# Two plain FFN blocks become a fourth group of seven products

## The chip, the core and the metric

The kernel runs on one core of a Trainium2 chip. The metric is the device time of one execution in microseconds (us), as the median of the runs. The engines are TensorE (PE: matmuls; PEld: its weight loads), VectorE (DVE), ScalarE (ACT), GpSimd (POOL) and SyncE (SP), which here only issues transfers. Each engine works through its own queue of instructions in the order in which the program put them there.

## What is computed

The reference is a trunk of two layers over 256 tokens of width 1024, in float32: a gated linear attention branch beside a grouped-query attention branch, a merge, then a SwiGLU feed-forward network (FFN) and a small embedding step, each with its norms. Cut to the FFN, which the change touches, with h of 256 x 1024 and a hidden width of 2816:

```python
u = rms_norm(h, g_ffn_pre)
gate, up = jnp.split(u @ w_ffn_in, 2, axis=-1)     # w_ffn_in: 1024 x 5632
h = h + rms_norm((jax.nn.silu(gate) * up) @ w_ffn_out, g_ffn_post)
```

## The kernel before

**Arithmetic.** Every float32 operand is held as two halves: a high half that TensorE takes (fp32r) and the remainder, the low half. A product of two operands is three matmuls: high by high, high by low, low by high (`mm3`, and the inner loop of `times`).

**The stream of weights.** Weights come in units of 1 MB (128 partitions x 2048 floats), in one list for the whole kernel, the *plan*. Class `Stream` handles them. `start` issues the next load on SyncE (L263) as soon as there is a place for it. `split` (L113, L109) makes the two halves, in two pieces each: a cast on ScalarE into `wh`, then on VectorE the subtraction that gives `wl`. The pool has four pairs of `wh` and `wl`; `fill` makes the next unit whenever fewer than four are held, and `done` gives a pair back when TensorE has used it.

**The FFN.** The hidden width is cut into 11 blocks of 256. A plain block is two units, one for each half of the rows, with the block's gate and up columns side by side; each takes 24 matmuls. Two blocks together can be done as a *group of seven products* (`seven`, L581): a scheme for 2 x 2 block matrices with seven half-sized products in place of eight, at the price of sums. A product is 12 matmuls, a group 84, two plain blocks 96. The sums on the activations are made once per layer (`sums`). The sums on the weights are made for every group, in `Stream.step`. With x, z, y and q the four units of a group:

- product 1 uses x; then VectorE adds z to x (L292) and a DMA adds y to z (L295)
- product 2 uses x; then VectorE adds y to x (L292)
- product 3 uses x; then two accumulating transfers issued by GpSimd add q, read from memory anew, to x (L308)
- products 4, 5, 6 and 7 use y, z, q and x

x and z are loaded straight into a `wh` and a `wl` buffer (tag `lent`), and so take one of the four pairs. They are loaded only after the previous group's product 7 has been made (`self.lend`, set in `step` for n = 7). y is loaded into another buffer, and q into a `raw` buffer like a plain unit, at the place of product 5 in the list of loads.

**Order.** A string sets the order of the units within the FFN, and the same string sets it in the plan: `u` is a unit of a plain block, a digit a product of a group, `o` a unit of `w_ffn_out` (24 matmuls, which need the hidden activations of that block, turned by a copy on ScalarE, a transposing transfer, another copy, and a cast with its low half), and `p` loads a gain and the embedding input, with no unit. PLAIN and PAIRS name the blocks (a pair by its first block; blocks 0 and 1 are done ahead of the string), OUT the order of the output units. The engines' queues follow from the order in which this code emits its instructions, with small tasks of other work woven in at ticks; when the program is built, instructions whose data allow it are also moved past one another, so the final queues are shown below where they matter.

The evictions of a group's products, by ScalarE's copies in `seven`, are L629 (product 1), L632 (product 2) and L634 (product 3); VectorE takes the later ones. `vmul` (L106) makes silu(gate) x up.

## Time and profile before

| | us |
|---|---|
| median of 3 runs | 918.69 |
| lowest and highest run | 918.22, 921.97 |
| the profiled execution | 921.25 |
| its span, first to last instruction | 919.1 |

The profile is of one execution. Its parts give the busy time of each engine, the chain of work that ended last (followed back from the last instruction through what released each step), the costliest groups of instructions, and the transfers. A timeline row has its start, its duration, the engine, the line of the kernel, the operation with output <- input, the count, and in brackets the idle time before it with what ended that. A name such as `wl_0ffnin` is the tile's tag and the part of the program: `0ffnin` is the FFN's first matrix in layer 0, `1ffnin` in layer 1. In rows with a count of 2 the duration runs over both.

### The profile page before, as it was taken

Reading aid. Unit: us, or ns where it says so; the run is one execution under the profiler, and the core shown is the slowest. Engines: PE = TensorE matmul, PEld = TensorE weight load, DVE = VectorE, ACT = ScalarE, POOL = GpSimd, SP = SyncE. Lnnn points to the kernel's source line nnn. Section 1 sums busy time; section 2 is a strip of 40 time slices with the busy share of each in tenths; the row PEclk is TensorE's granted clock in tenths of the full one; section 3 lists DMA queues with packets and bytes.
Section 4 is the critical chain, followed back from the end, with each engine's and each line's share of the span. In section 5 each row is a group of like instructions: output and inputs, shape, how many; then the busy total and the mean of one; then the engine's idle time right before and its main releaser. Section 6 shows DMA issues by size and latency. Waiting matters only on the chain.

```text
span 919.1 us, 12313 instructions
## 1 busy us (share of the span) xinstructions
PE 904.6 (98%) x4561; PEld 768.3 (84%) x4561; DVE 737.2 (80%) x947; ACT 643.9 (70%) x1032; POOL 112.4 (12%) x174
## 2 busy tenths in 40 slices
PE   8999999999999999999999999999999999999996
PEld 6999888888888888888899988888888788878786
DVE  4798987977679796888689789688786798968874
ACT  4658777964568796776665686878656787957663
POOL 2410201140010100010023002111001010101000
PEclk9999999999999999999999999999999999999999
DMA  6555356986489998966555524399675999979541
GB/s 218 182 193 180 117 163 231 229 241 234 144 243 256 279 273 250 301 194 240 184 176 184 190 91 148 128 290 234 208 247 173 274 230 290 261 284 243 200 167 46
DMA packets 123290, 193.38 MB, mean 210 GB/s; under 512 B 33431, under 2 KB 56471, under 8 KB 122206
## 3 DMA queue, kind: packets, MB, share of 16 engines
q1 hardware_dynamic: 117726, 175.81, 59.3%
q0 software_dynamic: 5504, 16.78, 10.1%
q8 instruction: 36, 0.59, 0.3%
q14 instruction: 24, 0.20, 0.1%
HBM read 175.80 MB, written 1.05 MB: 192 GB/s over the span
## 4 chain that ended last, share of the span: by engine, by line
PE 80%; ACT 6%; DMA 5%; DVE 4%; issue 2%; POOL 2%; SPq 0%; POOLq 0%; ACTq 0%; DVEq 0%
PE acc_0ffnin L97 10%; PE acc_1ffnin L97 10%; PE acc_0ffnin L581 5%; PE acc_1gate L97 5%; PE acc_0gate L97 5%; PE acc_1ffnin L581 4%; PE acc_1gqk L97 3%; PE acc_0rq L97 2%; PE acc_0gqk L97 2%; PE acc_1ple L97 2%; PE acc_1gg L97 2%; PE acc_0gg L97 2%; PE acc_0v L97 2%; PE acc_1v L97 2%; PE acc_1merge L97 2%; PE acc_0merge L97 2%
## 5 line engine op out<-in xcount | busy, mean ns | idle before, releaser
L97 PE MATMUL acc_1ffnin<-wh_1ffnin,big_1ffnin 128*128 128x512 f32 x176 | 56.5, 392 | 0.1
L97 PE MATMUL acc_0ffnin<-wh_0ffnin,big_0ffnin 128*128 128x512 f32 x176 | 56.2, 391 | 0.0
L109 DVE TENSOR_TENSOR wl_1ffnin<-raw_1ffnin,wh_1ffnin 128x1024 fp32r<-128x1024 f32 x38 | 44.9, 1220 | 12.3 <-ACT wh_1ffnin L113 12.3
L109 DVE TENSOR_TENSOR wl_0ffnin<-raw_0ffnin,wh_0ffnin 128x1024 fp32r<-128x1024 f32 x38 | 44.9, 1221 | 10.5 <-ACT wh_0ffnin L113 10.2
L113 ACT CAST wh_1ffnin<-raw_1ffnin 128x1024 fp32r<-128x1024 f32 x38 | 38.3, 1050 | 17.7 <-DMA raw_1ffnin<-in_w_ffn_out_dram 9.1
L113 ACT CAST wh_0ffnin<-raw_0ffnin 128x1024 fp32r<-128x1024 f32 x38 | 38.4, 1050 | 16.8 <-DMA raw_0ffnin<-in_w_ffn_out_dram 7.8
L109 DVE TENSOR_TENSOR wl_1ffnin<-lent_1ffnin,wh_1ffnin 128x1024 fp32r<-128x1024 f32 x30 | 35.5, 1220 | 4.9 <-ACT wh_1ffnin L113 4.7
L109 DVE TENSOR_TENSOR wl_0ffnin<-lent_0ffnin,wh_0ffnin 128x1024 fp32r<-128x1024 f32 x30 | 35.5, 1221 | 4.8 <-ACT wh_0ffnin L113 4.7
L97 PEld LDWEIGHTS acc_1ffnin<-wh_1ffnin,big_1ffnin 128*128 128x128 f32 x176 | 33.0, 188 | 7.2 <-ACT wh_1ffnin L113 0.5
L97 PEld LDWEIGHTS acc_0ffnin<-wh_0ffnin,big_0ffnin 128*128 128x128 f32 x176 | 33.0, 188 | 6.9 <-DVE big_0ffnin L109 0.2
L113 ACT CAST wh_1ffnin<-lent_1ffnin 128x1024 fp32r<-128x1024 f32 x30 | 30.3, 1049 | 8.6 <-issue 2.9
L113 ACT CAST wh_0ffnin<-lent_0ffnin 128x1024 fp32r<-128x1024 f32 x30 | 30.3, 1050 | 8.4 <-issue 2.9
L97 PE MATMUL acc_1ffnin<-wl_1ffnin,big_1ffnin 128*128 128x512 f32 x88 | 34.4, 391 | 0.8 <-DVE wl_1ffnin L109 0.8
L97 PE MATMUL acc_0ffnin<-wl_0ffnin,big_0ffnin 128*128 128x512 f32 x88 | 34.5, 392 | 0.3 <-DVE wl_0ffnin L109 0.3
L581 PE MATMUL acc_0ffnin<-wh_0ffnin,mid_0ffnin 128*128 128x512 f32 x96 | 31.0, 390 | 0.0
L581 PE MATMUL acc_1ffnin<-wh_1ffnin,mid_1ffnin 128*128 128x512 f32 x96 | 31.0, 390 | 0.0
L97 PE MATMUL acc_0ffnin<-wh_0ffnin,big_0wout 128*128 128x512 f32 x96 | 30.4, 389 | 0.0
L97 PE MATMUL acc_1ffnin<-wh_1ffnin,big_1wout 128*128 128x512 f32 x96 | 30.3, 389 | 0.0
L97 PE MATMUL acc_0rq<-wh_start,big_start 128*128 128x384 f32 (+1 forms) x96 | 25.4, 350 | 1.5 <-ACT big_start L124 1.5
L97 PE MATMUL acc_1rq<-wh_0ple,big_0ple 128*128 128x384 f32 (+1 forms) x96 | 23.5, 325 | 0.0
L581 PE MATMUL acc_1ffnin<-wh_1ffnin,big_1wout 128*128 128x512 f32 x72 | 23.1, 389 | 0.0
L581 PE MATMUL acc_0ffnin<-wh_0ffnin,big_0wout 128*128 128x512 f32 x72 | 23.1, 389 | 0.0
(745 smaller groups left out, 3011.7 us busy)
## 6 DMA issues: line engine op xcount, KB each, us to landing
raw_0ffnin<-in_w_ffn_out_dram SPq DMA_DIRECT2D x11, 1024.0 KB, 5.1
raw_1ffnin<-in_w_ffn_out_dram SPq DMA_DIRECT2D x11, 1024.0 KB, 5.1
lent_0ffnin<-in_w_ffn_in_dram SPq DMA_DIRECT2D x6, 1024.0 KB, 7.5
lent_1ffnin<-in_w_ffn_in_dram SPq DMA_DIRECT2D x6, 1024.0 KB, 6.0
raw_0rq<-in_w_in_dram SPq DMA_DIRECT2D x4, 1024.0 KB, 5.1
raw_0v<-in_w_in_dram SPq DMA_DIRECT2D x4, 1024.0 KB, 5.1
raw_0merge<-in_w_out_dram SPq DMA_DIRECT2D x4, 1024.0 KB, 5.2
raw_0wout<-in_w_ffn_in_dram SPq DMA_DIRECT2D x8, 512.0 KB, 4.6
```

The costliest lines, as they stand in the source:

```text
L97: return nc.tensor.matmul(o, lhsT, rhs, start=start, stop=stop)
L109: nc.vector.tensor_tensor(out=out, in0=in0, in1=in1, op=ALU.subtract)
L113: cast = nc.scalar.copy(hi, src)
L581: nc.tensor.matmul(o, x, y, start=first and k + n == 0, stop=k == 3 and n == 2, skip_group_check=not first)
```

## The change

Blocks 4 and 5 leave PLAIN and become a fourth pair, so that each layer's FFN has the groups of blocks 2, 4, 6 and 8 and one plain block, 10, at the start. Between product 7 of a group and product 1 of the next there is one `o` in the new string; in the old one there were two units, `uo` and `oo`. In the groups that are listed in ADDED (the first and the last one, "far" below, with the group of the attention's output matrix) the fourth sum stays with the accumulating transfers after product 3. In the two others ("near" below) VectorE adds q to x at product 5, from q's own `raw` buffer.

```diff
@@ -35,10 +35,11 @@
 
 
 
-FFN = "uu1u2u34u567" "uo12o34o5o67" "poo12o345o67"
+FFN = "uu12o34o567" "o123o4567" "po123o4567" "o123o4567"
 MERGE = "GGGG1G2G34G5G67gggg"
-PLAIN, PAIRS = (4, 5, 10), (2, 6, 8)
-OUT = (0, 1, 2, 3, 4, 5, 10, 6, 7, 8, 9)
+PLAIN, PAIRS = (10,), (2, 4, 6, 8)
+ADDED = (2, 8)
+OUT = (0, 1, 10, 2, 3, 4, 5, 6, 7, 8, 9)
 
 WAIT_LAST = (3, 4)
 SENT, LANDED, NEXT = 3, 9, 2
@@ -172,7 +173,7 @@
             )
         ]
 
-    plan = []
+    plan, added = [], []
     for l in range(DEPTH):
         w = a["w_in"][l]
         plan += [unit_rows(w, n, C_RA, C_RA + 1056, 2 if l + n == 0 else 1) for n in range(4)]
@@ -181,6 +182,7 @@
         gates = [unit(w, kh, c0) for c0 in (C_GA, C_GA + 512, C_GB, C_GB + 512) for kh in range(2)]
         glas = [unit(a["w_o_gla"][l], kh, j * 512) for j in range(2) for kh in range(2)]
         pair = [unit(a["w_o_attn"][l], kh, j * 512) for kh in range(2) for j in range(2)]
+        added.append(id(pair))
         for x in MERGE:
             plan.append(gates.pop(0) if x == "G" else glas.pop(0) if x == "g" else (pair, int(x)))
         plan += [unit(a["w_out"][l], kh, j * 512) for kh in range(2) for j in range(2)]
@@ -193,6 +195,8 @@
         for x in FFN.replace("p", ""):
             if x == "1":
                 pair = pairs.pop(0)
+                if PAIRS[-1 - len(pairs)] in ADDED:
+                    added.append(id(pair))
             plan.append(plains.pop(0) if x == "u" else outs.pop(0) if x == "o" else (pair, int(x)))
         plan += outs
         plan += [unit_rows(a["w_ple_proj"][l], 0)]
@@ -239,7 +243,7 @@
                         self.loads += [x, y, z]
                     if n == 5:
                         self.loads.append(q)
-                    self.jobs.append(lambda p=pairs[id(units)], n=n: self.step(n, *p))
+                    self.jobs.append(lambda p=pairs[id(units)], n=n, f=id(units) in added: self.step(n, f, *p))
 
         def lent(self, tag):
 
@@ -286,7 +290,7 @@
             for piece in self.put(x):
                 self.cast = split(*piece)
 
-        def step(self, n, x, y, z, q):
+        def step(self, n, far, x, y, z, q):
             def add(to, other):
                 c = slice(0, 2048)
                 nc.vector.tensor_tensor(out=to.raw[:, c], in0=to.raw[:, c], in1=other.raw[:, c], op=ALU.add)
@@ -302,10 +306,12 @@
                 sent(z, y.raw[:, :2048])
             elif n == 2:
                 add(x, y)
-            elif n == 3:
+            elif n == 3 and far:
                 for dst, src in q.make(x.raw):
                     for c in (slice(0, 2), slice(2, 4)):
                         nc.gpsimd.dma_start(dst[:, c], src[:, c], accum_op=ALU.add)
+            elif n == 5 and not far:
+                add(x, q)
             elif n == 7:
                 self.held -= 1
                 self.lend = True
```

VectorE's queue in layer 0, at the start of the second group: in the kernel before, from the low halves for product 1 on. (`wl<-lent` is a low half from x or z, `wl<-raw` one from a unit in `raw`, `lent<-lent` a sum, `big<-mid` a piece of the turned hidden activations.)

```order
L109 TENSOR_TENSOR wl_0ffnin_483_3093<-lent_0ffnin_470_3023,wh_0ffnin_482_3092 128x1024 x2
L106 TENSOR_TENSOR t512_0ffnin_480_3087<-mid_0ffnin_437_2814,t512_0ffnin_480_3087 128x512
L292 TENSOR_TENSOR lent_0ffnin_470_3023<-lent_0ffnin_470_3023,lent_0ffnin_472_3027 128x2048
L106 TENSOR_TENSOR t512_0ffnin_462_2982<-acc_0ffnin_463_2983,t512_0ffnin_462_2982 128x256
L106 TENSOR_TENSOR t512_0ffnin_462_2982<-acc_0ffnin_464_2984,t512_0ffnin_462_2982 128x256
L109 TENSOR_TENSOR wl_0ffnin_487_3129<-lent_0ffnin_470_3023,wh_0ffnin_486_3128 128x1024 x2
L292 TENSOR_TENSOR lent_0ffnin_470_3023<-lent_0ffnin_470_3023,big_0ffnin_471_3025 128x2048
L109 TENSOR_TENSOR wl_0ffnin_495_3172<-raw_0ffnin_473_3029,wh_0ffnin_494_3171 128x1024 x2
L109 TENSOR_TENSOR big_0ffnin_501_3196<-mid_0ffnin_484_3106,big_0ffnin_501_3196 128x4x128
L109 TENSOR_TENSOR wl_0ffnin_503_3201<-lent_0ffnin_470_3023,wh_0ffnin_502_3200 128x1024 x2
```

And in the changed kernel, from the same point on (L110 is the old L109, L107 the old L106, L296 the old L292):

```order
L110 TENSOR_TENSOR wl_0ffnin_469_3013<-lent_0ffnin_462_2975,wh_0ffnin_468_3012 128x1024 x2
L296 TENSOR_TENSOR lent_0ffnin_462_2975<-lent_0ffnin_462_2975,lent_0ffnin_464_2979 128x2048
L107 TENSOR_TENSOR t512_0ffnin_472_3037<-mid_0ffnin_437_2811,t512_0ffnin_472_3037 128x512
L110 TENSOR_TENSOR wl_0ffnin_475_3043<-lent_0ffnin_462_2975,wh_0ffnin_474_3042 128x1024 x2
L296 TENSOR_TENSOR lent_0ffnin_462_2975<-lent_0ffnin_462_2975,big_0ffnin_463_2977 128x2048
L110 TENSOR_TENSOR wl_0ffnin_479_3078<-lent_0ffnin_462_2975,wh_0ffnin_478_3077 128x1024 x2
L110 TENSOR_TENSOR wl_0ffnin_485_3101<-raw_0ffnin_465_2981,wh_0ffnin_484_3100 128x1024 x2
L110 TENSOR_TENSOR wl_0ffnin_488_3122<-big_0ffnin_463_2977,wh_0ffnin_487_3121 128x1024 x2
L110 TENSOR_TENSOR big_0ffnin_489_3140<-mid_0ffnin_476_3055,big_0ffnin_489_3140 128x4x128
L296 TENSOR_TENSOR lent_0ffnin_462_2975<-lent_0ffnin_462_2975,raw_0ffnin_466_2983 128x2048
L110 TENSOR_TENSOR wl_0ffnin_491_3145<-lent_0ffnin_464_2979,wh_0ffnin_490_3144 128x1024 x2
L110 TENSOR_TENSOR big_0ffnin_489_3140<-mid_0ffnin_477_3069,big_0ffnin_489_3140 128x4x128
```

The low halves for product 3 now stand ahead of those of the output unit (`wl<-raw`), not behind them, and the sum of x and q (`lent<-lent,raw`) stands between the two pieces of the turned activations that the output unit needs.

ScalarE's queue in layer 0, from the cast for product 2 to the eviction of product 2: in the kernel before, in the second group (COPY `mid<-acc` is an eviction, CAST `wh<-lent` a cast of x, `wh<-raw` of an output unit, COPY `mid<-mid` belongs to the turning):

```order
L113 CAST wh_0ffnin_486_3128<-lent_0ffnin_470_3023 128x1024 x2
L408 COPY t512_0ffnin_488_3139<-t512_0ffnin_462_2982 128x1024
L113 CAST wh_0ffnin_494_3171<-raw_0ffnin_473_3029 128x1024 x2
L427 COPY mid_0ffnin_484_3106<-mid_0ffnin_484_3106 128x2x512
L629 COPY mid_0ffnin_497_3179<-acc_0ffnin_499_3181 128x512
L113 CAST big_0ffnin_501_3196<-mid_0ffnin_484_3106 128x4x128
L113 CAST wh_0ffnin_502_3200<-lent_0ffnin_470_3023 128x1024 x2
L427 COPY mid_0ffnin_485_3120<-mid_0ffnin_485_3120 128x2x512
L632 COPY mid_0ffnin_497_3179<-acc_0ffnin_500_3182 128x512
```

And in the changed kernel, in the third group, from the cast for product 1 to the cast of the output unit (L114 is the old L113; L635 and L638 are the old L629 and L632):

```order
L114 CAST wh_0ffnin_504_3246<-lent_0ffnin_498_3209 128x1024 x2
L1345 ACTIVATE t512_0ffnin_508_3271<-acc_0ffnin_482_3085 128x512
L414 COPY t512_0ffnin_509_3274<-t512_0ffnin_508_3271 128x1024
L635 COPY mid_0ffnin_519_3322<-acc_0ffnin_521_3324 128x512
L114 CAST wh_0ffnin_510_3276<-lent_0ffnin_498_3209 128x1024 x2
L638 COPY mid_0ffnin_519_3322<-acc_0ffnin_522_3325 128x512
L114 CAST wh_0ffnin_517_3316<-lent_0ffnin_498_3209 128x1024 x2
L114 CAST wh_0ffnin_523_3339<-raw_0ffnin_501_3215 128x1024 x2
```

The eviction of product 1 stood behind the casts for product 2 and for the output unit and stands ahead of the cast for product 2 now; the eviction of product 2 stood behind the cast for product 3 and stands ahead of it now.

## The prediction

> **What bounds the kernel now.** I read the page's first and fourth parts first, then the busy time in windows inside layer 0's FFN, then its chain and timelines.

> ```profile
> PE 904.6 (98%) x4561; PEld 768.3 (84%) x4561; DVE 737.2 (80%) x947; ACT 643.9 (70%) x1032; POOL 112.4 (12%) x174
> PE 80%; ACT 6%; DMA 5%; DVE 4%; issue 2%; POOL 2%; SPq 0%; POOLq 0%; ACTq 0%; DVEq 0%
> ...
> 280.00:300.00 20.00, 20.00 (x90) 16.58 (x89) 19.22 (x22) 16.70 (x26) 0.95 (x1) 1.00 0.91 240
> 320.00:340.00 20.00, 20.00 (x90) 16.56 (x89) 19.50 (x20) 17.12 (x22) 0.88 (x1) 1.00 0.98 309
> ...
> 312.98 5.44 PE acc_0ffnin L97 x24
> 318.42 8.16 PE acc_0ffnin L581 x36
> 326.58 10.89 PE acc_0ffnin L97 x48
> ```

> TensorE is busy for 98% of the span and carries 80% of the chain. In the window rows (length, then busy time of PE, weight load, VectorE, ScalarE, GpSimd, then the granted clock) it never pauses, but VectorE beside it is at 19.22 and 19.50 of 20 us. So in the FFN the two stand almost level: TensorE is ahead only while VectorE's results come early enough. The chain's rows give the unit of the sum: 24 matmuls take 5.44 us, 0.227 each; a product of twelve takes 2.72. They also show the place: product 7 of the first group ends at 326.58, and **two** units, 10.89 us, lie between it and product 1 of the next.

> **What the change removes.** Per layer one more pair of blocks is done with 84 matmuls instead of 96: 24 fewer in two layers, 24 × 0.227 = 5.4 us less work for TensorE. Two accumulating transfers per near group, issued by GpSimd, go as well; they ran beside products 4 to 6 and only product 7 needs them, so I count nothing.

> **What it adds and moves.** Per layer: three more casts on ScalarE, three more low halves on VectorE, two sums that every group needs, and in the near groups (the two middle ones) the fourth sum. More important, only **one** unit now stands between product 7 and the next product 1, where the last two groups had two before. I therefore follow the weights of a next group from the end of the unit "o" that stands just ahead of product 5; call it E. In the old run that place was held by the unit ending at 318.42.

> ```profile
> 318.50 2.00 ACT L113 CAST wh_0ffnin<-lent_0ffnin 128x1024 fp32r<-128x1024 f32 x2 [2.87 <-issue]
> 327.31 1.99 ACT L113 CAST wh_0ffnin<-lent_0ffnin 128x1024 fp32r<-128x1024 f32 x2
> 334.11 2.00 ACT L113 CAST wh_0ffnin<-lent_0ffnin 128x1024 fp32r<-128x1024 f32 x2 [0.60 <-DVE lent_0ffnin L292]
> 340.63 0.58 ACT L629 COPY mid_0ffnin<-acc_0ffnin 128x512 f32<-128x512 f32 x1
> ...
> 319.59 2.36 DVE L109 TENSOR_TENSOR wl_0ffnin<-lent_0ffnin,wh_0ffnin 128x1024 fp32r<-128x1024 f32 x2 [2.33 <-ACT wh_0ffnin L113]
> 328.92 2.35 DVE L109 TENSOR_TENSOR wl_0ffnin<-lent_0ffnin,wh_0ffnin 128x1024 fp32r<-128x1024 f32 x2
> 331.19 0.69 DVE L106 TENSOR_TENSOR t_0ffnin<-mid_0ffnin,t_0ffnin 128x512 f32<-128x512 f32 x1
> 331.79 2.29 DVE L292 TENSOR_TENSOR lent_0ffnin<-lent_0ffnin,lent_0ffnin 128x2048 f32<-128x2048 f32 x1
> 335.19 2.36 DVE L109 TENSOR_TENSOR wl_0ffnin<-lent_0ffnin,wh_0ffnin 128x1024 fp32r<-128x1024 f32 x2 [0.45 <-ACT wh_0ffnin L113]
> 337.59 2.29 DVE L292 TENSOR_TENSOR lent_0ffnin<-lent_0ffnin,big_0ffnin 128x2048 f32<-128x2048 f32 x1
> 339.80 2.35 DVE L109 TENSOR_TENSOR wl_0ffnin<-raw_0ffnin,wh_0ffnin 128x1024 fp32r<-128x1024 f32 x2
> 342.07 0.69 DVE L109 TENSOR_TENSOR big_0ffnin<-mid_0ffnin,big_0ffnin 128x512 fp32r<-128x512 f32 x1
> ...
> 321.98 1.00 SPq L263 DMA_DIRECT2D lent_0ffnin<-in_w_ffn_in_dram  x2
> ```

> The first four rows are ScalarE's: the casts for products 7, 1 and 2, and the eviction of product 1. The cast for 7 starts at 318.50, when the unit's last matmul frees its slot. VectorE's rows follow: the low halves of 7, 1 and 2, the sums between them, the low halves of an output unit, and one piece of the turned hidden state. The last row is the load of the next x and z: 321.98, right behind the low halves of 7 (319.59 + 2.36 = 321.95). From these rows: cast and both low halves together take 334.11 to 337.55 = 3.44 us; the first low half is ready some 2.25 us behind a cast's start (1.08 until it begins, 1.2 for it); a pair of low halves costs VectorE 2.28 (339.80 to 342.07), a sum 2.28, a small product or a piece 0.61.

> The transfer of x has its own rows:

> ```profile
> lent_0ffnin<-in_w_ffn_in_dram SPq DMA_DIRECT2D x6, 1024.0 KB, 7.5
> lent_1ffnin<-in_w_ffn_in_dram SPq DMA_DIRECT2D x6, 1024.0 KB, 6.0
> DMA to landing us min/median/max: 5.4/8.3/13.6
> 367.97 0.92 SPq L263 DMA_DIRECT2D lent_0ffnin<-in_w_ffn_in_dram  x2
> 374.53 2.00 ACT L113 CAST wh_0ffnin<-lent_0ffnin 128x1024 fp32r<-128x1024 f32 x2
> ```

> The medians mix x with z and, in the third row, with accumulating transfers. x goes first, and its cast began 5.3 us (321.98 to 327.31) and 6.6 us (367.97 to 374.53) behind the issue. I take 6.0; the ends are 5.3 and 7.5.

> *The wait at products 1 to 3.* Counted from E: 7 is made at 3.45, x has landed at 9.45, the low halves of 1 are done at 12.9, a small product and the sum x+z end at 15.8, product 2's first low half is there at 18.05. TensorE has left after E: eight matmuls of 5 (four stand ahead of E), 6, 7 and one unit: 1.8 + 2.7 + 2.7 + 5.4 = 12.7; product 1 ends at 15.4 and 2 waits 2.65. ScalarE's new order says the same by another way: the cast for 2 stands behind the eviction of product 1, and that for 3 behind the eviction of product 2, so each product starts no earlier than 0.58 + 2.25 = 2.85 behind its forerunner's end. Before, whole units stood there for TensorE to do; now there is none. Two waits of 2.85: **5.7 us**, and product 3 begins at about E + 23.8.

> *The wait before the next E.* From the first low half of 3, VectorE still has, in its new order: the rest of 3 (1.1), the output unit (2.3), 4 (2.3), one piece (0.6), the new fourth sum (2.2), 5 (2.3), the second piece (0.6): 11.4 us. Behind that piece TensorE has 19 matmuls left to E, 4.3 us: 15.7 in all. Undelayed it would need products 3 and 4, the unit and four matmuls of 5: 2.7 + 2.7 + 5.4 + 0.9 = 11.8. **3.9 us** more, of which the new sum is 2.2. In this stretch VectorE is the bound.

> So one turn from a near group to the next costs 9.6 us. Each layer has two such turns (group 2 to 3, and 3 to 4): 4 × 9.6 = 38.4. The entry from group 1 to 2 has all of 5 behind E, so TensorE has 13.6 us there: product 2 waits 18.05 − 16.3 = 1.75, product 3 2.85: 4.6, twice. The far last group lacks the new sum, so its second part is some 2.3 us (its product 4 waits 1.8 for its first low half, the rest for the first piece), twice. Sum of the waits: 38.4 + 9.2 + 4.6 = 52.2. Against it stand 5.4 us of matmuls and about 1 us of waits in the old FFN that the new ones swallow, such as this:

> ```profile
> 362.44 0.50 PE L97 MATMUL acc_0ffnin<-wl_0ffnin,big_0ffnin 128*128 128x512 f32 x1 [0.27 <-DVE wl_0ffnin L109]
> ```

> Net: **+45.8 us**. The profiled execution took 921.25 us (919.1 of span and 2.1 around it), 2.6 above the median of 918.69; against it the sum is 967.1, and on the median's footing 964.5, which is my forecast. Its own range: with x at 5.3 or 7.5 instead of 6.0, the turns gain little, since the evictions hold 2 and 3 anyway, or lose up to 1.5 six times (+9); and the second part of a turn may be partly covered if VectorE's order leaves less on the path (half of it is 4 × 1.95 = 8). 950 to 976.

> **The rivals.**

> *The leads suffice (faster).* In the old run the low halves of product 1 were done at 331.27, 6.2 us before TensorE came to it at 337.47 (326.58 + 10.89); one unit less still leaves 0.8. For that product alone the lead suffices. If the same held for 2 and 3, only the 5.4 us would count: 913.3. Against it: the low halves of 3 were made last of all in the old order and had one whole unit more. 0.07. [...]

> *Some of both (within 0.5%, that is 4.6 us, about what a measurement of this kernel can tell from no change).* The waits would have to be a tenth of mine. 0.04.

> *Only VectorE's throughput counts (slower).* If its queue never waits for a load, a near group costs nine pairs of low halves, three sums and seven small ones: 20.5 + 6.6 + 4.3 = 31.4 us, with two waits for a cast 33.6, against 29.9 of TensorE (7 × 2.72 + 2 × 5.44). 4 × 3.7 − 6.4 = +8.4: 927. It would hold if the next x came so early that VectorE never waits for it; but the load is issued at 321.98, right behind 7's low halves, and VectorE has little else to do until it lands. 0.12.

> *Only the waits at products 1 to 3 stay*, the second part being covered: 4 × 5.7 + 2 × 4.6 − 6.4 = +25.6: 944. 0.12.

> *The clock falls in the waits.* At the kernel's end it did:

> ```profile
> 911.62 0.28 PE L97 MATMUL acc_1ple<-wh_1emb,big_1ffnout 128*128 128x256 f32 x1
> ...
> 914.00:915.00 1.00, 0.00 (x0) 0.00 (x0) 0.55 (x2) 0.00 (x0) 0.57 (x1) 0.86 0.00 0
> 915.00:916.00 1.00, 0.00 (x0) 0.00 (x0) 1.00 (x3) 0.00 (x0) 0.00 (x0) 0.50 0.00 0
> ```

> The last matmul ends at 911.90, and the mean of 0.86 puts the fall to half at 914.7, 2.8 us later, as long as my waits. If each of some twelve waits brought half speed for another 3 us, each cost 1.5: +18, 982. No wait of the old run inside the FFN reaches 1 us, so the trace can't decide. 0.10. [...]

> **How the numbers follow.** Forecast 0.55 (950 to 976), its rivals 0.12 (944), 0.12 (927), 0.10 (982), 0.04 (no change), 0.07 (faster). The range goes from 927 to 977: it leaves out the last three cases and the ends. Faster 0.07, same 0.04, slower 0.89.

> **What would show it.** Right: in groups 2 to 4 of both layers TensorE idles 2 to 3 us ahead of products 2 and 3, ended by VectorE's low halves; a turn takes 39 to 40 us; the x+q sum stands four times on VectorE; TensorE's busy time falls by 5 us while the span grows by 45; the chain's share of VectorE, ScalarE and DMA grows. Wrong: idle time ahead of product 1 beyond 1 us (the load is later than I took), a granted clock under 1.00 in the FFN's windows, or turns near 34 us. The forecast falls if the casts for 2 and 3 don't wait for the evictions.

## The result and the profile after

The changed kernel takes 963.54 us (961.3 to 965.1, 4 runs) against 919.61 for the kernel before in the same comparison; the ratio is 1.0473, with a 95% interval of 1.0439 to 1.0507. It is 43.9 us slower; the forecast was 45.8.

The page of the changed kernel, first and fourth part:

```profile
PE 921.3 (96%) x4537; PEld 769.7 (80%) x4537; DVE 772.2 (80%) x969; ACT 658.3 (69%) x1042; POOL 111.1 (12%) x172
...
PE 74%; DVE 8%; ACT 8%; DMA 5%; issue 3%; POOL 2%; SPq 0%; ACTq 0%; POOLq 0%; DVEq 0%
```

TensorE has 24 matmuls fewer, as it should, and is yet busy for 16.7 us *longer* (904.6 before). The chain's share of TensorE fell from 80% to 74%; VectorE's rose from 4% to 8%, ScalarE's from 6% to 8%. All of the loss lies in the FFN: from its first matmul to its last (accumulators `acc_0ffnin`, `acc_1ffnin`) the timeline has 198.7 and 200.1 us, against 176.4 and 178.0 before, together 44.4 more. The waits of TensorE by what ended them (total, times, longest) show where:

```profile
PE acc_0ffnin L587 <- ACT wh_0ffnin L114: 8.7, 5, 2.0
PE acc_1ffnin L587 <- ACT wh_1ffnin L114: 8.7, 5, 2.0
PE acc_0ffnin L587 <- DVE wl_0ffnin L110: 5.7, 8, 1.5
PE acc_1ffnin L587 <- DVE wl_1ffnin L110: 4.2, 7, 0.8
```

L587 is the groups' line. These are 27.3 us in four rows; the same view of the kernel before has no row of the groups' line. One of the waits, in the timeline of layer 0 from the first to the third product of the third group: TensorE (its first row is product 1's first matmul), then ScalarE's evictions and casts, then VectorE's sums and low halves.

```profile
361.10 0.39 PE L587 MATMUL acc_0ffnin<-wh_0ffnin,big_0wout 128*128 128x512 f32 x1
...
365.60 0.51 PE L587 MATMUL acc_0ffnin<-wh_0ffnin,mid_0ffnin 128*128 128x512 f32 x1 [1.62 <-ACT wh_0ffnin L114]
366.86 0.50 PE L587 MATMUL acc_0ffnin<-wl_0ffnin,mid_0ffnin 128*128 128x512 f32 x1 [0.32 <-DVE wl_0ffnin L110]
371.45 0.50 PE L587 MATMUL acc_0ffnin<-wh_0ffnin,mid_0ffnin 128*128 128x512 f32 x1 [1.81 <-ACT wh_0ffnin L114]
372.71 0.50 PE L587 MATMUL acc_0ffnin<-wl_0ffnin,mid_0ffnin 128*128 128x512 f32 x1 [0.76 <-DVE wl_0ffnin L110]
...
364.02 0.58 ACT L635 COPY mid_0ffnin<-acc_0ffnin 128x512 f32<-128x512 f32 x1 [1.25 <-PE acc_0ffnin L587]
364.50 2.00 ACT L114 CAST wh_0ffnin<-lent_0ffnin 128x1024 fp32r<-128x1024 f32 x2
369.68 0.58 ACT L638 COPY mid_0ffnin<-acc_0ffnin 128x512 f32<-128x512 f32 x1 [3.18 <-PE acc_0ffnin L587]
370.36 1.99 ACT L114 CAST wh_0ffnin<-lent_0ffnin 128x1024 fp32r<-128x1024 f32 x2
...
361.60 2.29 DVE L296 TENSOR_TENSOR lent_0ffnin<-lent_0ffnin,lent_0ffnin 128x2048 f32<-128x2048 f32 x1
365.58 2.36 DVE L110 TENSOR_TENSOR wl_0ffnin<-lent_0ffnin,wh_0ffnin 128x1024 fp32r<-128x1024 f32 x2 [1.69 <-ACT wh_0ffnin L114]
367.97 2.29 DVE L296 TENSOR_TENSOR lent_0ffnin<-lent_0ffnin,big_0ffnin 128x2048 f32<-128x2048 f32 x1
```

The cast for product 2 (364.50) stands right behind the eviction of product 1, and behind the sum x+z that ends at 363.89. The cast for product 3 (370.36) stands behind the eviction of product 2 and the sum x+y, which ends at 370.26. Products 2 and 3 each start when their own cast has just been made.

Another part is a lower granted clock. The windows of the changed kernel are cut here at the times at which the granted clock changes, 3.41 us apart (columns as in the prediction; the number behind PE's busy time counts the matmuls that reach into the window):

```profile
327.15:330.56 3.41, 2.75 (x11) 1.91 (x11) 2.71 (x3) 1.50 (x3) 0.00 (x0) 1.00 1.11 216
330.56:333.98 3.42, 0.84 (x3) 0.19 (x1) 2.25 (x2) 2.73 (x4) 0.00 (x0) 1.00 0.89 168
333.98:337.39 3.41, 3.20 (x8) 2.53 (x9) 3.41 (x4) 3.41 (x4) 0.00 (x0) 0.50 0.00 0
368.11:371.52 3.41, 1.60 (x8) 1.01 (x6) 2.24 (x2) 1.75 (x3) 0.00 (x0) 1.00 0.76 154
402.24:405.66 3.42, 1.05 (x3) 0.67 (x4) 1.96 (x3) 2.48 (x3) 0.85 (x1) 1.00 0.87 170
405.66:409.07 3.41, 3.41 (x9) 2.64 (x8) 2.82 (x2) 0.00 (x0) 0.00 (x0) 0.50 1.05 214
409.07:412.48 3.41, 1.02 (x4) 0.31 (x3) 1.40 (x2) 2.96 (x4) 0.00 (x0) 1.00 0.01 0
412.48:415.90 3.42, 3.42 (x9) 2.65 (x10) 3.42 (x4) 3.42 (x5) 3.15 (x3) 0.50 0.34 31
...
801.60:805.02 3.42, 1.39 (x6) 0.68 (x4) 2.26 (x2) 2.05 (x3) 0.00 (x0) 1.00 1.03 194
835.74:839.15 3.41, 1.47 (x9) 0.74 (x7) 1.73 (x3) 2.48 (x3) 0.86 (x1) 1.00 0.96 191
842.56:845.98 3.42, 1.42 (x5) 0.57 (x4) 0.90 (x1) 2.46 (x4) 0.00 (x0) 1.00 0.14 26
876.70:880.11 3.41, 1.84 (x7) 1.32 (x8) 2.59 (x3) 1.70 (x2) 0.86 (x1) 1.00 0.93 182
880.11:883.52 3.41, 1.61 (x8) 1.02 (x6) 2.25 (x2) 1.84 (x3) 0.00 (x0) 1.00 0.84 171
```

In layer 0 a window at half clock stands behind each one in which TensorE is busy for 0.84 to 1.05 us; behind 1.60 us (368.11) none does. In layer 1 the clock also falls behind windows with 1.39, 1.42, 1.47 and 1.61 us, and stays behind 1.84. In the windows at half clock a matmul was issued every 0.427 us and not every 0.227. Summed over the FFN's matmuls in such windows this is 12.6 us of stretch (4.4 in layer 0, 8.2 in layer 1); before there was none.

The waits and the stretch, 27.3 and 12.6 us, are 39.9 of the 49.8 that have to be explained (44.4, and the 5.4 that 24 matmuls less should have saved). Some 4 us more belong to the 25 waits of the rows: idle time is counted from the end of the last matmul's row, 0.39 us behind its start, but the next one would have started 0.227 behind it. The remaining 6 lie in shorter delays, which were not followed.

### The profile page after: what moved, and what is told of

It is laid out like the page before. It is cut to its first block, busy times and chain, and to the rows that moved or that the text cites. A ratio compares the mean times of both kernels' runs of the same rounds, so it can differ in the third digit from the quotient of the medians.

```text
span 960.8 us, 12294 instructions
## 1 busy us (share of the span) xinstructions
PE 921.3 (96%) x4537; PEld 769.7 (80%) x4537; DVE 772.2 (80%) x969; ACT 658.3 (69%) x1042; POOL 111.1 (12%) x172
## 3 DMA queue, kind: packets, MB, share of 16 engines
HBM read 173.70 MB, written 1.05 MB: 182 GB/s over the span
## 4 chain that ended last, share of the span: by engine, by line
PE 74%; DVE 8%; ACT 8%; DMA 5%; issue 3%; POOL 2%; SPq 0%; ACTq 0%; POOLq 0%; DVEq 0%
PE acc_1ffnin L98 8%; PE acc_1ffnin L587 6%; PE acc_0ffnin L98 6%; PE acc_1gate L98 5%; PE acc_0gate L98 5%; PE acc_0ffnin L587 4%; ACT wh_0ffnin L114 3%; PE acc_1gqk L98 2%; PE acc_0gqk L98 2%; PE acc_1ple L98 2%; PE acc_0gg L98 2%; PE acc_1gg L98 2%; PE acc_1v L98 2%; PE acc_0v L98 2%; PE acc_1merge L98 2%
## 5 line engine op out<-in xcount | busy, mean ns | idle before, releaser
L110 DVE TENSOR_TENSOR wl_1ffnin<-lent_1ffnin,wh_1ffnin 128x1024 fp32r<-128x1024 f32 x40 | 47.3, 1221 | 18.3 <-ACT wh_1ffnin L114 18.3
L110 DVE TENSOR_TENSOR wl_0ffnin<-lent_0ffnin,wh_0ffnin 128x1024 fp32r<-128x1024 f32 x40 | 47.3, 1221 | 18.3 <-ACT wh_0ffnin L114 18.3
L587 PE MATMUL acc_1ffnin<-wh_1ffnin,mid_1ffnin 128*128 128x512 f32 x128 | 48.2, 444 | 8.7 <-ACT wh_1ffnin L114 8.7
L587 PE MATMUL acc_0ffnin<-wh_0ffnin,mid_0ffnin 128*128 128x512 f32 x128 | 45.5, 422 | 8.7 <-ACT wh_0ffnin L114 8.7
L114 ACT CAST wh_1ffnin<-lent_1ffnin 128x1024 fp32r<-128x1024 f32 x40 | 40.2, 1048 | 11.0 <-DVE lent_1ffnin L296 4.9
L114 ACT CAST wh_0ffnin<-lent_0ffnin 128x1024 fp32r<-128x1024 f32 x40 | 40.2, 1048 | 10.8 <-DVE lent_0ffnin L296 4.5
L587 PEld LDWEIGHTS acc_1ffnin<-wh_1ffnin,mid_1ffnin 128*128 128x128 f32 x128 | 28.4, 222 | 17.2 <-ACT wh_1ffnin L114 11.2
L114 ACT CAST wh_0ffnin<-raw_0ffnin 128x1024 fp32r<-128x1024 f32 x32 | 32.2, 1049 | 12.1 <-PE acc_0ffnin L98 3.6
L114 ACT CAST wh_1ffnin<-raw_1ffnin 128x1024 fp32r<-128x1024 f32 x32 | 32.2, 1049 | 12.0 <-PE acc_1ffnin L587 4.2
L110 DVE TENSOR_TENSOR wl_1ffnin<-raw_1ffnin,wh_1ffnin 128x1024 fp32r<-128x1024 f32 x32 | 37.9, 1220 | 2.4 <-ACT wh_1ffnin L114 2.3
L110 DVE TENSOR_TENSOR wl_0ffnin<-raw_0ffnin,wh_0ffnin 128x1024 fp32r<-128x1024 f32 x32 | 37.9, 1220 | 2.3 <-ACT wh_0ffnin L114 2.3
L587 PEld LDWEIGHTS acc_0ffnin<-wh_0ffnin,mid_0ffnin 128*128 128x128 f32 x128 | 26.3, 206 | 16.4 <-ACT wh_0ffnin L114 11.0
L587 PE MATMUL acc_1ffnin<-wl_1ffnin,mid_1ffnin 128*128 128x512 f32 x64 | 29.8, 465 | 4.3 <-DVE wl_1ffnin L110 4.2
L587 PE MATMUL acc_0ffnin<-wl_0ffnin,mid_0ffnin 128*128 128x512 f32 x64 | 28.2, 441 | 5.7 <-DVE wl_0ffnin L110 5.7
L587 PE MATMUL acc_1ffnin<-wh_1ffnin,big_1wout 128*128 128x512 f32 x96 | 31.4, 389 | 0.0
L587 PE MATMUL acc_0ffnin<-wh_0ffnin,big_0wout 128*128 128x512 f32 x96 | 31.4, 389 | 0.0
## 6 DMA issues: line engine op xcount, KB each, us to landing
raw_0ffnin<-in_w_ffn_out_dram SPq DMA_DIRECT2D x11, 1024.0 KB, 6.5
raw_1ffnin<-in_w_ffn_out_dram SPq DMA_DIRECT2D x11, 1024.0 KB, 5.0
lent_0ffnin<-in_w_ffn_in_dram SPq DMA_DIRECT2D x8, 1024.0 KB, 5.3
lent_1ffnin<-in_w_ffn_in_dram SPq DMA_DIRECT2D x8, 1024.0 KB, 7.0
raw_0rq<-in_w_in_dram SPq DMA_DIRECT2D x4, 1024.0 KB
raw_0v<-in_w_in_dram SPq DMA_DIRECT2D x4, 1024.0 KB, 5.0
raw_0merge<-in_w_out_dram SPq DMA_DIRECT2D x4, 1024.0 KB
```

Source lines behind the costliest of these rows:

```text
L110: nc.vector.tensor_tensor(out=out, in0=in0, in1=in1, op=ALU.subtract)
L114: cast = nc.scalar.copy(hi, src)
L587: nc.tensor.matmul(o, x, y, start=first and k + n == 0, stop=k == 3 and n == 2, skip_group_check=not first)
```

## The experiments

All ratios are to the kernel before, with 95% intervals. The changed kernel's is 1.0473 (1.0439 to 1.0507).

| run | us | ratio |
|---|---|---|
| e1 all fourth sums by transfers | 968.42 | 1.0528 (1.0502 to 1.0554) |
| e2 two units between the groups | 942.74 | 1.0254 (1.0226 to 1.0281) |
| e3 both | 940.74 | 1.0230 (1.0205 to 1.0256) |
| e4 zero matmuls in the waits | 958.75 | 1.0422 (1.0404 to 1.0440) |
| e5 kernel before, one unit between | 929.65 | 1.0108 (1.0082 to 1.0134) |
| e6 next x loaded from product 6 on | 952.78 | 1.0360 (1.0344 to 1.0376) |
| e7 e2 and e6 | 949.56 | 1.0317 (1.0290 to 1.0343) |
| e8 e3 and e6 | 946.44 | 1.0296 (1.0275 to 1.0317) |
| e9 fourth sum left out in the near groups | 967.87 | 1.0531 (1.0503 to 1.0559) |
| e10 e1 with product 4 ahead of the unit | 963.25 | 1.0467 (1.0439 to 1.0495) |
| e11 e10 and e6 | 952.09 | 1.0351 (1.0328 to 1.0374) |

**The distance between two groups (e2, e5).** e2 moves an output unit on the changed kernel, e5 moves a unit the other way on the kernel before:

```diff
-FFN = "uu12o34o567" "o123o4567" "po123o4567" "o123o4567"
+FFN = "uu12o34567" "oo1234567" "poo1234567" "oo12o34567"
...
-FFN = "uu1u2u34u567" "uo12o34o5o67" "poo12o345o67"
+FFN = "uu1u2u34u567" "o12uo34o5o67" "po12oo345o67"
```

> The output unit that stood between products 3 and 4 goes in front of the next product 1 (two units between product 7 and product 1 again); four groups and VectorE's fourth sums stay. Theory (the distance from the release of product 7's buffer to products 1 to 3 is too short by one unit): product 7's buffer is now freed by the end of product 4, TensorE has 24.5 us of work from there to product 3, whose first low half is ready after 23.8; the waits at products 2 and 3 vanish, about 1.7 us a turn stay ahead of product 4 (VectorE: rest of 3, the sum, a piece, 4), the clock stays at 1.00: 925, between 918 and 935. Rival (VectorE's throughput is the bound, the place does not matter): above 945.

> The kernel before with its three groups and all its work; only one unit of each later group is moved from in front of product 1 to the place behind product 2, so that one unit, not two, stands between product 7 and the next product 1. Theory (the distance alone makes the waits): product 2 waits 1.75 us in each of the four entries, product 3 nothing, since two units stand ahead of it: +4 to +8, 923 to 928. Rival (the waits of the changed kernel come from a busier VectorE, the distance alone costs nothing): 918 to 921.

e2 takes 942.74 us: one unit's place is worth 20.8 us of the 43.9. The waits at products 2 and 3 shrink, though they do not vanish, and only two windows at half clock are left in the FFN, where the changed kernel has nine: 16 matmuls in place of 66, so up to 10 us of the 20.8 can be stretch that is gone. But a new wait comes, ahead of product 4. The timeline of e2, TensorE, then ScalarE:

```profile
332.42 0.49 PE L587 MATMUL acc_0ffnin<-wh_0ffnin,mid_0ffnin 128*128 128x512 f32 x1 [0.45 <-ACT wh_0ffnin L114]
338.68 0.50 PE L587 MATMUL acc_0ffnin<-wh_0ffnin,mid_0ffnin 128*128 128x512 f32 x1 [2.21 <-ACT mid_0ffnin L638]
...
333.22 1.35 ACT L433 COPY mid_0ffnin<-mid_0ffnin 128x1024 uint16<-128x1024 uint16 x1
334.44 1.04 ACT L114 CAST wh_0ffnin<-big_0ffnin 128x1024 fp32r<-128x1024 f32 x1
335.39 0.61 ACT L114 CAST big_0ffnin<-mid_0ffnin 128x512 fp32r<-128x512 f32 x1
335.91 1.04 ACT L114 CAST wh_0ffnin<-big_0ffnin 128x1024 fp32r<-128x1024 f32 x1
336.86 1.33 ACT L433 COPY mid_0ffnin<-mid_0ffnin 128x1024 uint16<-128x1024 uint16 x1
338.06 0.57 ACT L638 COPY mid_0ffnin<-acc_0ffnin 128x512 f32<-128x512 f32 x1
```

Product 4 sums onto the accumulator of product 2, whose eviction (338.06) stands on ScalarE behind two turning copies and the casts. Without the unit between products 3 and 4 nothing covers that: 2.2 us in each of the four turns. A wait of 1.7 was expected there, from VectorE's queue; that the eviction makes it was not foreseen. It is only a part of what e2 takes beyond the 918 to 935 expected: the groups' other waits still add up to 5.0 us, and 3.3 are new, for the low halves of output units.

e5 takes 9.8 us more than the kernel before, with the same work on every engine: the theory's direction, and more than its size (4 to 8; 923 to 928 us). In its third group the waits stand as predicted for product 2, and also at product 1, since x, whose load was issued at 366.33, was cast at 376.60 only (whether the load held the cast or ScalarE's copy ahead of it, the trace does not tell):

```profile
366.33 0.92 SPq L263 DMA_DIRECT2D lent_0ffnin<-in_w_ffn_in_dram  x2
...
376.60 1.99 ACT L113 CAST wh_0ffnin<-lent_0ffnin 128x1024 fp32r<-128x1024 f32 x2
...
377.69 0.49 PE L581 MATMUL acc_0ffnin<-wh_0ffnin,big_0wout 128*128 128x512 f32 x1 [0.51 <-ACT wh_0ffnin L113]
383.49 0.50 PE L581 MATMUL acc_0ffnin<-wh_0ffnin,mid_0ffnin 128*128 128x512 f32 x1 [1.75 <-ACT wh_0ffnin L113]
```

So in that kernel the distance alone costs about 10 us, without any fourth group and without a fourth sum on VectorE. The rival of a busier VectorE is out as the sole cause.

**The sum on VectorE (e1, e3, e9, e10).** e1 gives the middle groups their sum by transfers, e9 leaves it out there, e10 is e1 with product 4 ahead of the output unit in the string; e3 is e2 with e1's edit.

```diff
-ADDED = (2, 8)
+ADDED = (2, 4, 6, 8)
...
-            elif n == 5 and not far:
-                add(x, q)
...
-FFN = "uu12o34o567" "o123o4567" "po123o4567" "o123o4567"
+FFN = "uu12o34o567" "o1234o567" "po1234o567" "o1234o567"
```

> All four groups make the fourth sum by accumulating transfers, none on VectorE. Theory of the prediction (the wait before the next E is VectorE's queue between the first low half of product 3 and the second piece, of which the new sum is 2.2 us): each of the four turns is 2.2 us shorter, 963.5 - 9 = about 954, and the turns fall from 39 to about 37 us. Rival (the turn is set by the load and the evictions alone, and VectorE's sum is covered): no change, 961 to 965. Second rival (the accumulating transfers land too late for product 7's cast): slower than 965, with product 7 waiting for a transfer.

> The changed kernel with the fourth sum left out in the two middle groups (neither VectorE nor a transfer adds q to x, so product 7 uses a sum without q there). The build gives TensorE the same order as in the run with all sums by transfers: the tail of product 4 behind the output unit. Theory (in that run the gain of VectorE's sum was lost to the order, since the casts for 6 and 7 then both start behind the output unit): as slow as that run, 965 to 969. Rival (the accumulating transfers cost the time there, by landing late or by their share of the queues): 952 to 957, since here there are none in the middle groups.

> All fourth sums by accumulating transfers, and product 4 ahead of the output unit in the string, so that product 4's pair is free before the unit ends and only product 7's cast waits for the unit. Theory of the order: the 1.9 us of one cast per turn come back, and with them VectorE's missing sum shows: 952 to 960. Rival (the order is not what held that run): 965 to 970.

> As the run with two units between, and all fourth sums by accumulating transfers. Theory: VectorE has 2.2 us less per near group, so nothing is left of the wait ahead of product 4, and the 5.4 us of saved matmuls are seen: 913 to 920. Rival (the accumulating transfers, two per group more, are late for product 7, which is now made earlier): above 925, with product 7 or its cast waiting for a transfer.

e1 is slower by some 5 us, not faster by 9. The prediction's price of 2.2 us a turn for the sum did not come back. Its second rival, late transfers, was the first suspicion; e9 has none in the middle groups and is as slow (967.87), so it falls. What the two share is TensorE's order, and through it ScalarE's. The casts for products 6 and 7 in the changed kernel, in e1 and in e9:

```profile
345.63 2.01 ACT L114 CAST wh_0ffnin<-raw_0ffnin 128x1024 fp32r<-128x1024 f32 x2 [1.98 <-DVE big_0ffnin L110]
348.35 2.01 ACT L114 CAST wh_0ffnin<-lent_0ffnin 128x1024 fp32r<-128x1024 f32 x2 [0.71 <-PE acc_0ffnin L98]
```

```profile
348.26 2.01 ACT L114 CAST wh_0ffnin<-raw_0ffnin 128x1024 fp32r<-128x1024 f32 x2 [3.14 <-PE acc_0ffnin L98]
350.17 2.00 ACT L114 CAST wh_0ffnin<-lent_0ffnin 128x1024 fp32r<-128x1024 f32 x2
```

```profile
349.55 2.01 ACT L114 CAST wh_0ffnin<-raw_0ffnin 128x1024 fp32r<-128x1024 f32 x2 [3.15 <-PE acc_0ffnin L98]
351.46 2.00 ACT L114 CAST wh_0ffnin<-lent_0ffnin 128x1024 fp32r<-128x1024 f32 x2
```

In the changed kernel product 4 ends ahead of the output unit, product 6's cast starts at 345.63, and only product 7's waits for the unit (348.31). In e1 and e9 the build puts the tail of product 4 behind the unit; now product 6's cast waits for the unit, and 7's stands behind it, 1.9 us later. All that follows, the load of the next x first, is 1.9 us later, and what VectorE gained is lost. With product 4 in front, in e10, 7's cast starts at the unit's end again, and 5.2 us come back (963.25). They do not bring it under the changed kernel; 952 to 960 was expected. Part of that is the lower clock: 86 of the FFN's matmuls are at half clock in e1's trace and 88 in e10's, against 66 in the changed kernel's, and 20 more are 4 us of stretch. Without the stretch (0.2 us for each such matmul) the four turns, from one product 1 to the next, add up to 146.0 us in the changed kernel, 145.3 in e1 and 141.9 in e10: some 1 us a turn for e10, where 2.2 was priced, and e10's order differs too. So no run is faster for taking the sum off VectorE in this order, and in the order of e2 the difference is 2 us (e3), inside the intervals, where 913 to 920 was expected of e3 and 925 of e2. Of the other mechanism in e3's row, transfers that land late for product 7, its waits show nothing; product 2's eviction stays first (4.4 and 4.3 us).

**The lower clock (e4).**

```diff
+            nc.tensor.matmul(o, zero, rhs, start=first, stop=False, skip_group_check=True)
...
+        pad(sp, v, True, idle)
         times(v, form(0), True, lambda: nc.scalar.copy(p5, v))
         yield
+        pad(sp, a, False, idle)
```

> The changed kernel with seven matmuls of a zero operand (1.6 us) ahead of products 2 and 3 in groups 2 to 4 of each layer, accumulated onto the same sums, so that TensorE is not idle there. If the lower granted clock costs what its matmuls were stretched by (12.6 us in the trace of the changed kernel) and it comes from the low activity: granted clock near 1.00, 963.5 - 12.6 + about 2 for the matmuls that find no idle time = 953. If the stretched matmuls lie beside waits for VectorE: clock near 1.00 and no gain, 961 to 966. If the clock falls for another reason: clock 0.98 and 963 to 967.

The granted clock is 0.999, against 0.983 in the changed kernel, and no window inside the FFN is at half. The time is 958.75, some 5 us less. So in this kernel the clock fell because TensorE did too little in some windows (it was busy for 0.84 to 1.61 of their 3.41 us). The 5 us are what is left behind the padding's own cost: its 84 matmuls are 19 us of TensorE's time, of which only a part fell into idle time. The price of the lower clock thus lies between these 5 us and the 12.6 of stretch, part of which may lie beside other waits; no run settles it.

**Loading x earlier (e6, e7, e8, e11).** The next x and z may be loaded as soon as product 6 is made, so that they take a pair ahead of product 7:

```diff
-            elif n == 7:
                 self.held -= 1
+            if n == 6:
                 self.lend = True
```

> The changed kernel with one rule of the stream changed: the next group's x and z may be loaded once product 6 has been made, into another of the four pairs, not only behind product 7. Theory (the chain release, product 7, load, product 1, sums sets the turn): the load is issued up to 3.4 us earlier, counted from the release, and the four turns and two entries get shorter by 2 to 3 us each: 945 to 952. Rival (with two pairs lent the other units find no pair): casts of 7 and of the output unit come later, no gain or slower, above 962.

> Two units between product 7 and product 1 (as in the second run) and x and z loaded from product 6 on. In the second run some 1 us a turn is left ahead of product 3, ended by casts and low halves, and 2.2 us ahead of product 4, ended by product 2's eviction on ScalarE. Theory: the first goes, the second stays: 937 to 940. Rival (pairs too short): above 943.

> As the run before, with all fourth sums by accumulating transfers: 935 to 939 by the theory, above 941 by the rival.

> As the run before, and x and z of the next group loaded from product 6 on, which gained 10.7 us on the changed kernel. If the two gains lie on one chain and add up: 942 to 950. If they are gains on the same stretch: as the better of the two, 951 to 955. Neither comes near the kernel before, whose groups have twice the other work between them.

On the changed kernel this gains 10.8 us, near the expected 945 to 952: in e6 the load of x is issued at 347.8 and that of z at 351.0, when the unit ends; in the changed kernel x's was issued 3.5 us behind the unit's end. Product 2 of the third and fourth groups no longer waits for its cast. Product 3 still does, for 2.0 us, and its cast follows the sum x+y, which ends 0.2 us behind the eviction of product 2. The load is thus part of the loss, but a part only. With two units between (e7, e8) the rule costs 6 to 7 us instead of gaining, as the rival said: in e7 the FFN's casts wait 12.8 us for matmuls of a group to end, against 6.2 in e2, and TensorE waits about 1 us at each of six output units. In e11 the rule and e10's order give what e6 gives alone: gains on the same stretch. No version with four groups comes near the kernel before.

## Why the prediction was right, and where it was not

- *Right: the place and the mechanism.* The waits stand ahead of products 2 and 3 in the later groups of both layers, with none at product 1; they end with casts and low halves. A turn, from one product 3 to the next, took 38.5 and 39.7 us in layer 0 (332.93, 371.45, 411.10) and 40.5 and 38.3 in layer 1, against 39.5 forecast. e2 shows that the place of one unit is worth about half of the loss, and e5 that the shorter distance costs time in the old kernel too.
- *Wrong in part: the wait before the next E.* 3.9 us was forecast for a near group, 2.2 of it for the sum. The changed kernel's timeline of the third group, VectorE's low halves of 3, TensorE's wait at product 4, and the chain's row of the unit's end; then, from the second group, VectorE's second piece and TensorE's first matmuls that came after it:

```profile
371.43 2.36 DVE L110 TENSOR_TENSOR wl_0ffnin<-lent_0ffnin,wh_0ffnin 128x1024 fp32r<-128x1024 f32 x2 [1.17 <-ACT wh_0ffnin L114]
377.26 0.51 PE L587 MATMUL acc_0ffnin<-wl_0ffnin,mid_0ffnin 128*128 128x512 f32 x1 [1.50 <-DVE wl_0ffnin L110]
...
384.85 1.82 PE acc_0ffnin L98 x8
...
344.95 0.68 DVE L110 TENSOR_TENSOR big_0ffnin<-mid_0ffnin,big_0ffnin 128x512 fp32r<-128x512 f32 x1
346.34 0.84 PE L98 MATMUL acc_0ffnin<-wh_0ffnin,big_0ffnin 128*128 128x512 f32 x3
```

  From the first low half of 3 (371.43 + 1.2 = 372.6) to E (386.67) are 14.0 us, 2.2 more than the 11.8 undelayed; 1.5 of them is the wait for product 4's first low half. In the other three turns no such wait stands there, and TensorE's delay behind product 3, without the stretch, is 0.3 to 1.0 us. The failing step is that TensorE has all 19 matmuls left "behind that piece". Four of the output unit's matmuls use only the high half of the piece, which ScalarE's cast makes, and seven belong to products 4 and 5. In the second group these eleven ran from 343.70 to 346.34, and VectorE's piece (344.95 to 345.63) was ready when the last eight came. The sum stood ahead of that piece, so its 2.2 us were covered there. Without the stretch its absence gave at most some 1 us a turn, in e10.
- *Right in size: the waits at products 1 to 3.* 5.7 us were forecast. In the third group 11.61 us lie between product 1's first matmul (361.10) and the first that uses product 3's low half (372.71). 25 matmuls at 0.227 and four small ones at 0.11 are 6.1 of them, so TensorE was held up for 5.5. (The idle times in the rows are less, 4.5, for the reason given above.) The other three turns give 5.5 to 6.0 without the stretch, the two entries 4.6 and 5.0 against 4.6. Less sure is what holds the casts. The forecast named the evictions; in the eight casts of the turns the eviction ended last in six, by 0.5 to 1.6 us, and together with VectorE's sum in two, and in e6 the sum ended last at product 3. So an earlier eviction alone could bring the casts forward by no more than these 0.5 to 1.6 us; no run tried it.
- *Underrated: the clock.* It was a rival with a chance of 0.10, priced at 18 us, and the forecast itself has no term for it. It came in nine windows of 3.41 us with 12.6 us of stretch; e4 puts its price at 5 us or more. Two signs that the prediction itself had named came out against it: the granted clock fell in the FFN, and TensorE's busy time rose by 16.7 us where it should have fallen by 5, mostly by the stretch. The 2.8 us that the prediction read at the kernel's end, from the last matmul to the fall, did not carry over: the longest pause of TensorE in the FFN was 2.03 us (ahead of 804.65), and it was busy for 0.84 to 1.61 us of the windows behind which the clock fell. The 3 us at half speed behind each of some twelve waits, in the rival's price, were the author's estimate; the trace has 3.41 or 6.83 us at a time, seven times.
- *Luck: the total.* Counted from matmul to matmul, the waits at products 1 to 3 come to 32 us in the trace, as forecast; the waits behind product 3 to 6.6 where 20.2 were forecast; and the stretch at half clock to 13 (12.6 in the count above), where the forecast had none. The sum is 52, and 52.2 was forecast. So 45.8 met 43.9 because one term that was too high and one that was left out were about equal. The waits alone are nearer to the rival of 944, in which the second part is covered.
- *The rivals.* The leads did not suffice: their step was product 1, where it held, and it failed at 2 and 3. VectorE's throughput alone (927) is out: VectorE itself idled 1.69 us ahead of product 2's low halves (365.58) and 1.17 ahead of product 3's (371.43), waiting for casts.

What stays open: the half of the loss that e2 leaves, 23 us, was followed to product 2's eviction (8.7 us in its waits) but not to the end, and no run moved an eviction. The price of the lower clock is known only to lie between 5 and 12.6 us. How long the load of x takes is open as well: of the casts from which the prediction read its 6.0 us, the one at 327.31 began without idle time on ScalarE, and so did the one in the changed kernel (357.65, 5.8 us behind the issue), so these two are upper bounds.

## What to carry to other kernels

Fewer operations on a busy engine can be worth nothing where each group also has a fixed chain (release a buffer, load, cast, sum, cast) that other work must cover: here every group went from 4.7 units of other work to 2.5 (14 units for three groups, 10 for four). So price a denser schedule by that chain, from the event that frees its first buffer, and not by busy times. And an experiment that removes work also lets the build reorder: compare the queues before reading its time.
